# Two-layer decoder trunk on one core: four closing blocks of 512 columns, shared early chunks, and a residual in written order

## The chip, the cores and the metric

The kernel runs on one core of a Trainium2 chip. The metric is device time in microseconds (us) of one execution; a lower number is better.

## The reference, cut to what matters

The reference is a decoder trunk of two layers over 256 rows of 2048 numbers. Each layer adds three sub-layers to the running sum `h`: a token mixing, a cross attention over 256 memory rows, and a gated feed-forward. Each sub-layer normalises its input and its output.

```python
D_MODEL, SEQ, DEPTH, MEM_LEN = 2048, 256, 2, 256
FFN_HIDDEN = 5632

def rms_norm(x, g):
    xf = x.astype(jnp.float32)
    y = xf * lax.rsqrt(jnp.mean(xf * xf, axis=-1, keepdims=True) + EPS)
    return (y * g.astype(jnp.float32)).astype(x.dtype)
```

Of a layer, in words: `mix` is three groups of attention heads and a gating, joined to 2048 columns and multiplied by `w_out` (2048 by 2048); then `h = h + rms_norm(mix, mix_post_g)`. The cross attention takes keys and values from the normalised memory (`x_wkv`), queries from `rms_norm(h, x_pre_g)`, four heads of 128, and closes with `x_wo` (512 by 2048); then `h = h + rms_norm(cross, x_post_g)`. The feed-forward is `silu(h w_g) * (h w_u)` with 5632 hidden columns, closes with `f_w_down` (5632 by 2048), and is added in the same manner.

## The kernel before, in words

Every float32 product is computed as three products of a 32-bit format with a shorter mantissa: each operand is split into a part `hi` (ScalarE copies it, L206) and a rest `lo` (VectorE subtracts, L207), and PE, the matmul engine, adds hi·hi, hi·lo and lo·hi. Weights come by DMA from SyncE's queue into three buffers `raw` of 1 MB. `splits()` cuts each into **chunks** of 1024 columns, of which `hi` and `lo` have three buffers each. One chunk of a 512-column block holds two row groups `k` of 128, and gives 24 matmuls of 256 columns where the weights stand still (`mm_t`), or 12 of 512 where the activations do (`mm_n`).

`weights()` (L358) hands out chunks. After each it calls `prefetch()`, which writes out the splits of later chunks, so that up to three are in hand, and `pump()`, which advances every generator in `side` by one step: that is how the normalisations and attentions are laid beside the matmuls. The order on an engine is set by a scheduler's own estimate of time, save within `tc.manual_schedule(engines={DVE, ACT})`, where VectorE (DVE) and ScalarE (ACT) take the order in which the code is written and PE is still placed by the estimate. `begin(gen, n, at)` (L638) opens that mode at step `at` of a generator's first `n` steps; it ends with the block of weights that is being read. In that mode `pump()` comes before `prefetch()` (L371 to L375).

The closing projections `w_out`, `x_wo` and `f_w_down` run over `TAIL`, five blocks of columns, with two accumulators each. The first block of `w_out` takes its row groups in the order `MIX_FIRST`: first the ten that exist early (`m6`, and columns 6 and 7), then six whose mixing outputs are split late by `chunks()` into `mx`.

`residual()` (L585) follows a closing projection: it evaluates the last block's squares (`evac`), takes the inverse root of the row sums (`row_rsqrt`, on DVE), adds the scaled block to `H` (`add`, L604), transposes pairs of 128-column groups of `H` on PE (`turn_x`, tile `xtp`), and splits them into the next sub-layer's `x` (`split_x`: `hi` by L212 on ACT, `lo` by L213 on DVE). With `bare` false (after the mixing) it runs beside the matmuls of the memory's keys, `acc<-mh,...` and `acc<-ml,...`: 8 chunks K0 to K7 of 24 matmuls, after which the query matmuls Q0 to Q7 need `x`. There the order is the scheduler's, and half of the sums go to ACT and POOL (`beside`). With `bare` true (after cross attention and feed-forward) warming matmuls stand first, and DVE and ACT run in the written order.

```python
            if ramp:
                pump()
                prefetch()
                ...
            else:
                prefetch(3 if not hold or n < nk else 2)
                pump()
```

Of the kernel before, what the change touches and what calls it, by code (L numbers as in the profile page):

```python
# [10 lines left out]
F32 = mybir.dt.float32  # L11
# [10 lines left out]
P = 128  # L22
# [36 lines left out]
def trunk(ctx: ExitStack, tc, a, onehot, out):  # L59
# [14 lines left out]
    ps3 = ctx.enter_context(tc.tile_pool(name="ps3", bufs=2, space=PSUM))  # L74


    nc.gpsimd.memset(pc.tile([P, 8], F32, name="half_pc"), 0.0)


    ident = cp.tile([P, P], F32, name="ident")  # L80
# [175 lines left out]

        return lambda k0, n: w3d[k0 * P:(k0 + n) * P, :, c0:c0 + cols].rearrange("(k p) c f -> p k c f", p=P)

    TAIL = ((0, 512), (512, 512), (1024, 512), (1536, 256), (1792, 256))
    MIX_FIRST = ((8, 4), (0, 4), (6, 2), (4, 2), (12, 4))  # L260

    def plan():


        def spec(dram, nk, cols, loads=None, sub=None):
            per = 2048 // cols
            loads = loads or [(k, min(per, nk - k)) for k in range(0, nk, per)]
            return dram, nk, cols, loads, sub or (4 if cols <= 256 else 2 if cols <= 512 else 1)

        for l in range(L):  # L270
            w_in, w_out = a["w_in"][l], a["w_out"][l]
            w_qi = a["b_w_qidx"][l].rearrange("r g d -> r (g d)")
            w_uq = a["b_w_uq"][l].rearrange("r h d -> r (h d)")
            w_uk = a["b_w_uk"][l].rearrange("r h d -> r (h d)")
            w_uv = a["b_w_uv"][l].rearrange("r h d -> r (h d)")
            x_wkv = a["x_wkv"][l].rearrange("k c h e -> k c (h e)")
            x_wq = a["x_wq"][l].rearrange("k h e -> k (h e)")
            x_wo = a["x_wo"][l].rearrange("h e d -> (h e) d")
            yield spec(rows(w_in, C_CU, 512), KD, 512, None if l else [(0, 1), (1, 3), (4, 4), (8, 4), (12, 4)])
# [12 lines left out]
            w_qk = w_in[:, 0:1536].rearrange("k (c f) -> k c f", c=2)  # L292
            for h in range(0, 6, 2):
                yield spec(pairs(w_qk, h * P, 256), KD, 512)
            yield spec(rows(w_in, C_CV, 512), KD, 512)
            for i, (c0, n) in enumerate(TAIL):
                yield spec(rows(w_out, c0, n), KD, n, MIX_FIRST if i == 0 else None)
            yield spec(rows(x_wkv[:, 0, :], 0, 512), KD, 512)
            yield spec(rows(x_wq, 0, 512), KD, 512)
            for g in range(2):  # L300
                yield spec(rows(x_wkv[:, 1, :], g * 256, 256), KD, 256)
            for c0, n in TAIL:
                yield spec(rows(x_wo, c0, n), 4, n, None, 2)
            nh = FH // P // 2
            for hf in range(2):
                for j in range(0, nh, 2):
                    yield spec(pairs(a["f_w_gu"][l], (hf * nh + j) * P, 256), KD, 512)
                wd = a["f_w_down"][l][hf * nh * P:(hf + 1) * nh * P, :]
                for c0, n in TAIL:
                    yield spec(rows(wd, c0, n), nh, n)  # L310
# [85 lines left out]
                mm(outs[b], hi[:, cs[b]], xl[k], False, last)  # L396
        return tiles

    def mm_n(nk, cols, xh, xl, hold=False):

        xh, xl = ([x[:, k, :] for k in range(nk)] if not isinstance(x, list) else x for x in (xh, xl))
        tiles = [acc.tile([P, 512], F32, tag="acc", name="acc") for _ in range(2)]
        for n, k, hi, lo in weights(nk, cols, hold):
            for t in range(2):
                o = tiles[t][:, :cols]
                h, lw = xh[k][:, t * P:(t + 1) * P], xl[k][:, t * P:(t + 1) * P]
                mm(o, h, hi, n == 0, False)
                mm(o, h, lo, False, False)
                mm(o, lw, hi, False, n == nk - 1)
        return tiles  # L410

    def warm(n):
# [172 lines left out]
    def residual(og, ss, evac, nxt, res, bare, off):  # L585
# [5 lines left out]
        r = row_rsqrt(ss)  # L591
        if bare:
            warm(38)
        yield
        res["x"] = xh, xl, _ = new_x("x", off)

        def add(c, n, beside=False):
            f = slice(c * P, (c + n) * P)
            for t in range(2):
                if beside:  # L600
                    nc.scalar.activation(og[:, t, f], og[:, t, f], AF.Copy, scale=r[:, t:t + 1])
                    nc.gpsimd.tensor_tensor(H[:, t, f], H[:, t, f], og[:, t, f], op=ALU.add)
                else:
                    nc.vector.scalar_tensor_tensor(H[:, t, f], og[:, t, f], r[:, t:t + 1], H[:, t, f],  # L604
                                                   op0=ALU.mult, op1=ALU.add)

        def turn(c):
            split_x(turn_x(H, c), c, xh, xl, nxt)


        add(0, 2)
        p = turn_x(H, 0)
# [1 line left out]
        split_x(p, 0, xh, xl, nxt)  # L614
        turn(2)
        add(4, 2)
        if bare:
            prefetch()
        rest()
        add(6, 2)  # L620
        yield
        turn(4)
        yield
        turn(6)
        add(8, 4, not bare)
        yield
        turn(8)
        yield
        turn(10)
        add(12, 4, not bare)  # L630
        yield
        turn(12)
        yield
# [11 lines left out]
            next(gen)  # L645
        start(gen)

    def project_out(nk, xh, xl, og, gain, add=False, first=None):

# [3 lines left out]
        for g, (c0, cols) in enumerate(TAIL):  # L653
            last = g == len(TAIL) - 1
            if gain.shape[0] == P:
                gb = gain[:, c0:c0 + cols]
            else:
                gb = wk.tile([P, 512], F32, tag="gb", name="gb", bufs=2)[:, :cols]
                nc.gpsimd.dma_start(gb, gain[c0:c0 + cols].partition_broadcast(P))
            tiles = mm_n(nk, cols, *(first if first and g == 0 else (xh, xl)), hold=last)  # L660

            def evac(tiles=tiles, g=g, c0=c0, cols=cols, gb=gb, last=last):
                for t in range(2):
                    d, p = og[:, t, c0:c0 + cols], tiles[t][:, :cols]
                    if add:
                        nc.vector.tensor_tensor(d, p, d, op=ALU.add)
                        square(d, ss[:, t, g:g + 1])
                        if not last:
                            nc.gpsimd.tensor_tensor(d, d, gb, op=ALU.mult)
                    else:  # L670
                        square(p, ss[:, t, g:g + 1])
                        if not last:
                            nc.vector.tensor_tensor(d, p, gb, op=ALU.mult)
                if not last:
                    return

                def rest():
                    for t in range(2):
                        d, p = og[:, t, c0:c0 + cols], tiles[t][:, :cols]
                        if add:  # L680
                            nc.gpsimd.tensor_tensor(d, d, gb, op=ALU.mult)
                        else:
                            nc.vector.tensor_tensor(d, p, gb, op=ALU.mult)
                return rest
            if last:
                return ss, evac
            later(evac)

    def last_residual(og, ss, evac):
# [5 lines left out]
        for t, f in pieces[:3]:  # L695
            summed[t, f.start] = p = acc.tile([P, 512], F32, tag="acc", name="hsum")
            mm(p, ident, H[:, t, f], True, False)
        dg = spread(r)
        rest()
        for t, f in pieces[:3]:  # L700
            mm(summed[t, f.start], dg[:, t, :], og[:, t, f], False, True)
        for i in (3, 0, 4, 1, 5, 2, 6, 7):
            t, f = pieces[i]
            p = summed.get((t, f.start))
            if p is not None:
                nc.scalar.activation(H[:, t, f], p, AF.Copy)
# [22 lines left out]
    in_raw.append(next(loads))  # L729
    fetch_x(256, 256)  # L730
    in_raw.append(next(loads))
    fetch_x(512, 512)
    in_raw.append(next(loads))
    warm(12)
    for _ in g0:
        pass
    cur = {}
    begin(initial(cur), 2, -1)


    for l in range(L):
# [377 lines left out]
        og = xp.tile([P, 2, D], F32, tag="x", name="og")  # L1119
        pool = {}  # L1120

        at = used[0]

        def turn_memory():
            while used[0] == at or any(g.__name__ in ("last_heads", "chunks") for g in side):
# [4 lines left out]
            pool["m"] = mh, ml = [kp.tile([P, KD, S], F32R, name=n) for n in ("mh", "ml")]  # L1130
            yield from memory(kp, mh, ml, l)
        start(turn_memory())
        oss, evac = project_out(KD, mxx[:, 0], mxx[:, 1], og, a["mix_post_g"][l], first=first)


        kp = pool["kp"]
# [3 lines left out]
        kX = kp.tile([P, 4, 256], F32, name="kX")  # L1140
        vX = kp.tile([P, 2, 512], F32, name="vX")
        nx = {}
        begin(residual(og, oss, evac, ("x_pre_g", l), nx, False, 64), 2, -1)
        t_k = mm_t(KD, [P] * 4, mh, ml)

        def k_out():
# [142 lines left out]
```

## Time and profile before

| | us |
|---|---|
| median of three runs | 2426.8 |
| lowest and highest | 2422.76, 2428.68 |
| the profiled execution's own time | 2425.12 |
| its span, first to last instruction | 2423.4 |
| PE busy in it | 2389.2 (99%) |
| DVE, ACT, POOL busy | 1412.6, 1188.7, 201.9 |

The busy share of PE is modelled from the starts of pipelined matmuls, so the distance between starts tells more than a duration: a row `start us, us, ... xN [idle before <-releaser]` gives the first start of N like instructions in a row, and how long the engine had been idle before it and for whom.

### The profile page before, as it was taken

How to read it: one execution, taken by the hardware profiler on the slowest of the kernel's cores; microseconds unless marked ns; L12 is line 12 of the kernel's file. 1: busy time of each engine (PE TensorE's matmuls, PEld its weight loads, DVE VectorE, ACT ScalarE, POOL GpSimd, SP SyncE). 2: the span in 40 equal slices, each digit the busy share in tenths (PEclk: the TensorE clock that was granted, in tenths of full speed). 3: DMA queues.
4: the chain of work that ended last, by engine and by line, in shares of the span. 5: the costliest groups of instructions: out<-in, count | busy, mean ns of one | idle time of the engine just before them, and what ended most of it. 6: DMA issues, size and time to landing. Idle time of an engine off the chain costs nothing.

```text
span 2423.4 us, 42616 instructions
## 1 busy us (share of the span) xinstructions
PE 2389.2 (99%) x17741; PEld 2249.2 (93%) x17741; DVE 1412.6 (58%) x2129; ACT 1188.7 (49%) x1764; POOL 201.9 (8%) x177
## 2 busy tenths in 40 slices
PE   9999999999999999999999999999999999999998
PEld 8899789999998999998999997999999989999987
DVE  5686766665554455555466767666655544555554
ACT  5655545554444444444455655455544444444443
POOL 0010131000000000000100102100000000000001
PEclk9999999999999999999999999999999999999999
DMA  7755475455655565555554555644555555555553
GB/s 250 242 170 157 164 252 176 157 176 196 197 195 194 187 195 193 192 192 192 190 173 132 187 156 189 219 157 157 190 194 192 191 192 190 192 195 196 193 191 131
DMA packets 356757, 453.27 MB, mean 187 GB/s; under 512 B 11290, under 2 KB 275412, under 8 KB 356052
## 3 DMA queue, kind: packets, MB, share of 16 engines
q1 hardware_dynamic: 354836, 443.45, 55.9%
q0 software_dynamic: 1248, 6.29, 0.8%
q8 instruction: 139, 2.28, 0.4%
q10 hardware_dynamic: 480, 0.80, 0.1%
q14 instruction: 54, 0.44, 0.1%
HBM read 444.72 MB, written 5.79 MB: 186 GB/s over the span
## 4 chain that ended last, share of the span: by engine, by line
PE 91%; DVE 4%; ACT 2%; DMA 2%; issue 1%; SPq 0%; POOL 0%; ACTq 0%; POOLq 0%; DVEq 0%
PE acc L201 86%; DVE lo L207 2%; ACT hi L206 1%; PE xtp L564 1%; PE ixp L201 1%; ACT sqj L550 1%; PE lga L201 1%; DMA m<-in_mem_dram 1%; DVE H L604 1%; DMA H<-in_x_dram 0%; DVE mx L207 0%; PE warm L416 0%; DMA lp<-in_a_lambda_dram 0%; PE pvb L201 0%; PE lgx L201 0%
## 5 line engine op out<-in xcount | busy, mean ns | idle before, releaser
L207 DVE TENSOR_TENSOR lo<-raw,hi 128x1024 fp32r<-128x1024 f32 (+2 forms) x839 | 1000.9, 1194 | 870.7 <-ACT hi L206 868.4
L206 ACT ACTIVATE hi<-raw 128x1024 fp32r<-128x1024 f32 (+2 forms) x839 | 861.0, 1027 | 1037.7 <-PE acc L201 954.7
L201 PE MATMUL acc<-x,hi 128*128 128x256 f32 (+1 forms) x7360 | 1270.0, 277 | 0.0
L201 PEld LDWEIGHTS acc<-x,hi 128*128 128x128 f32 (+1 forms) x7360 | 1111.2, 188 | 2.8 <-issue 2.7
L201 PE MATMUL acc<-x,lo 128*128 128x256 f32 x3680 | 889.5, 278 | 6.8 <-DVE lo L207 4.6
L201 PEld LDWEIGHTS acc<-x,lo 128*128 128x128 f32 x3680 | 690.1, 188 | 13.4 <-DVE lo L207 6.1
L201 PE MATMUL acc<-hi,hx 128*128 128x512 f32 (+1 forms) x1760 | 452.6, 347 | 0.0
L201 PEld LDWEIGHTS acc<-hi,hx 128*128 128x128 f32 x1760 | 308.5, 189 | 41.7 <-issue 0.2
L201 PE MATMUL acc<-lo,hx 128*128 128x512 f32 (+1 forms) x880 | 304.9, 347 | 0.0
L201 PEld LDWEIGHTS acc<-lo,hx 128*128 128x128 f32 x880 | 166.7, 189 | 20.5 <-issue 0.2
L1243 POOL TENSOR_TENSOR g<-g,u 128x512 f32<-128x512 f32 x44 | 76.6, 1741 | 1131.3 <-ACT g L1241 1131.3
L201 PE MATMUL acc<-hi,mx 128*128 128x512 f32 (+1 forms) x576 | 148.1, 345 | 7.9 <-DVE mx L207 4.0
L201 PEld LDWEIGHTS acc<-hi,mx 128*128 128x128 f32 x576 | 99.6, 190 | 21.8 <-DVE mx L207 5.1
L201 PE MATMUL acc<-hi,x 128*128 128x384 f32 (+1 forms) x384 | 109.3, 360 | 0.0
L201 PE MATMUL acc<-lo,mx 128*128 128x512 f32 (+1 forms) x288 | 98.4, 343 | 0.1
L201 PEld LDWEIGHTS acc<-hi,x 128*128 128x128 f32 x384 | 70.1, 188 | 8.3 <-issue 3.3
L201 PE MATMUL acc<-lo,x 128*128 128x384 f32 (+1 forms) x192 | 69.7, 363 | 0.0
L212 ACT ACTIVATE x<-xtp,gT 128x256 fp32r<-128x256 f32 x96 | 39.5, 470 | 48.7 <-PE xtp L564 48.7
L201 PEld LDWEIGHTS acc<-lo,mx 128*128 128x128 f32 x288 | 54.6, 190 | 7.0 <-DVE lo L207 1.0
L213 DVE SCALAR_TENSOR_TENSOR x<-xtp,gT,x 128x256 fp32r<-128x256 f32 x96 | 41.6, 478 | 16.1 <-ACT x L212 15.9
L201 PE MATMUL acc<-hi,cx 128*128 128x512 f32 (+1 forms) x160 | 42.7, 352 | 0.0
L201 PEld LDWEIGHTS acc<-lo,x 128*128 128x128 f32 x192 | 36.1, 188 | 3.9 <-issue 1.3
(247 smaller groups left out, 1878.4 us busy)
## 6 DMA issues: line engine op xcount, KB each, us to landing
raw<-in_f_w_gu_dram SPq DMA_DIRECT2D x352, 512.0 KB, 4.5
raw<-in_f_w_down_dram SPq DMA_DIRECT2D x76, 1024.0 KB, 5.1
raw<-in_w_out_dram SPq DMA_DIRECT2D x30, 1024.0 KB, 5.4
raw<-in_w_in_dram SPq DMA_DIRECT2D x48, 512.0 KB, 4.7
raw<-in_w_in_dram SPq DMA_DIRECT2D x23, 1024.0 KB, 5.3
raw<-in_x_wkv_dram SPq DMA_DIRECT2D x16, 1024.0 KB, 4.9
raw<-in_w_in_dram SPq DMA_DIRECT2D x12, 960.0 KB, 5.1
raw<-in_x_wq_dram SPq DMA_DIRECT2D x8, 1024.0 KB, 5.2
```

Source lines behind the costliest of these rows:

```text
L201: return nc.tensor.matmul(o, lhsT=lhsT, rhs=rhs, start=start, stop=stop, skip_group_check=True)
L206: nc.scalar.activation(hi, src, AF.Copy)
L207: eng.tensor_tensor(lo, src, hi.bitcast(F32), op=ALU.subtract)
L212: nc.scalar.activation(hi, src, AF.Copy, scale=scale)
L213: nc.vector.scalar_tensor_tensor(lo, src, scale, hi.bitcast(F32), op0=ALU.mult, op1=ALU.subtract)
L550: nc.scalar.activation(q[:, :src.shape[-1]], src, AF.Square, accum_out=red)
L564: nc.tensor.transpose(p[:, t * P:(t + 1) * P], src[:, t, (c + j) * P:(c + j + 1) * P], ident)
L604: nc.vector.scalar_tensor_tensor(H[:, t, f], og[:, t, f], r[:, t:t + 1], H[:, t, f], op0=ALU.mult, op1=ALU.add)
L1243: nc.gpsimd.tensor_tensor(g, g, u, op=ALU.mult)
```

## The change: what it does

There are six edits. `TAIL` has four blocks of 512 instead of three of 512 and two of 256. The first two blocks of `w_out` run their ten early row groups one after the other, and then their six late ones, on four accumulators; the memory's transposes begin one block later. In `mm_n`, the last two row groups of a projection's last block run first for rows 0 to 127, then for 128 to 255. `residual()` after the mixing runs in written order: the last block's gain first, then for each of eight pairs the sum, the transposes and the split, one pair a step; the share of ACT and POOL is gone. `initial()`, which splits the input, runs in written order too, and the first weights come in smaller loads, three of them ahead of `H`'s third part. The last block's gain is multiplied on DVE. Some paddings change, by which `cx` and small work tiles move within SBUF.

```diff
-    TAIL = ((0, 512), (512, 512), (1024, 512), (1536, 256), (1792, 256))
-    MIX_FIRST = ((8, 4), (0, 4), (6, 2), (4, 2), (12, 4))
+    TAIL = ((0, 512), (512, 512), (1024, 512), (1536, 512))
+
+    MIX_EARLY, MIX_LATE = ((8, 4), (0, 4), (6, 2)), ((4, 2), (12, 4))
...
-            yield spec(rows(w_in, C_CU, 512), KD, 512, None if l else [(0, 1), (1, 3), (4, 4), (8, 4), (12, 4)])
+            yield spec(rows(w_in, C_CU, 512), KD, 512, None if l else [(0, 1), (1, 1), (2, 2), (4, 4), (8, 4), (12, 4)])
...
-            for i, (c0, n) in enumerate(TAIL):
-                yield spec(rows(w_out, c0, n), KD, n, MIX_FIRST if i == 0 else None)
+            for part, n in ((MIX_EARLY, 10), (MIX_LATE, 6)):
+                for c0, cols in TAIL[:2]:
+                    yield spec(rows(w_out, c0, cols), n, cols, part)
+            for c0, cols in TAIL[2:]:
+                yield spec(rows(w_out, c0, cols), KD, cols)
...
+        end = []
+        for w in weights(nk, cols, hold):
+            if hold and w[0] >= nk - 2:
+                end.append(w)
+                if w[0] < nk - 1:
+                    continue
+                for t in range(2):
+                    for w in end:
+                        step(t, *w)
+            else:
+                for t in range(2):
+                    step(t, *w)
...
         r = row_rsqrt(ss)
         if bare:
             warm(38)
-        yield
+            yield
         res["x"] = xh, xl, _ = new_x("x", off)
 
-        def add(c, n, beside=False):
+        def add(c, n):
             f = slice(c * P, (c + n) * P)
             for t in range(2):
-                if beside:
-                    nc.scalar.activation(og[:, t, f], og[:, t, f], AF.Copy, scale=r[:, t:t + 1])
-                    nc.gpsimd.tensor_tensor(H[:, t, f], H[:, t, f], og[:, t, f], op=ALU.add)
-                else:
-                    nc.vector.scalar_tensor_tensor(H[:, t, f], og[:, t, f], r[:, t:t + 1], H[:, t, f],
-                                                   op0=ALU.mult, op1=ALU.add)
+                nc.vector.scalar_tensor_tensor(H[:, t, f], og[:, t, f], r[:, t:t + 1], H[:, t, f],
+                                               op0=ALU.mult, op1=ALU.add)
...
+        if not bare:
+            rest()
+            yield
+            for c in range(0, KD, 2):
+                add(c, 2)
+                turn(c)
+                yield
+            yield from pre_norm(res)
+            return
...
+        warm(24)
         dg = spread(r)
-        rest()
...
     in_raw.append(next(loads))
+    in_raw.append(next(loads))
     fetch_x(512, 512)
-    in_raw.append(next(loads))
...
-    begin(initial(cur), 2, -1)
+    begin(initial(cur), 2, 0)
...
-        oss, evac = project_out(KD, mxx[:, 0], mxx[:, 1], og, a["mix_post_g"][l], first=first)
+        early = [mm_n(10, cols, *first, more=True) for _, cols in TAIL[:2]]
+        oss, evac = project_out(KD, mxx[:, 0], mxx[:, 1], og, a["mix_post_g"][l], early=early)
...
-        begin(residual(og, oss, evac, ("x_pre_g", l), nx, False, 64), 2, -1)
+        begin(residual(og, oss, evac, ("x_pre_g", l), nx, False, 64), 1, 0)
...
-        cx = kp.tile([P, 2080], F32R, name="cx")[:, 32:].rearrange("p (a h t) -> p a h t", a=2, h=4)
+        cx = kp.tile([P, 2064], F32R, name="cx")[:, 16:].rearrange("p (a h t) -> p a h t", a=2, h=4)
```

Three places in the order of instructions follow. On DVE beside the memory's keys, before (`H` is the sum, `x` the split's rest of a transposed half pair, `lo` the rest of a weight chunk):

```order
L604 SCALAR_TENSOR_TENSOR H<-og,rs_r,H 128x256 x8
L207 TENSOR_TENSOR lo<-raw,hi 128x1024 x2
L213 SCALAR_TENSOR_TENSOR x<-xtp,gT,x 128x256 x4
L207 TENSOR_TENSOR lo<-raw,hi 128x1024 x2
L213 SCALAR_TENSOR_TENSOR x<-xtp,gT,x 128x256 x4
L207 TENSOR_TENSOR lo<-raw,hi 128x1024
```

and after:

```order
L694 TENSOR_TENSOR og<-acc,gb 128x512 x2
L619 SCALAR_TENSOR_TENSOR H<-og,rs_r,H 128x256 x2
L213 SCALAR_TENSOR_TENSOR x<-xtp,gT,x 128x256 x2
L207 TENSOR_TENSOR lo<-raw,hi 128x1024
L619 SCALAR_TENSOR_TENSOR H<-og,rs_r,H 128x256 x2
L213 SCALAR_TENSOR_TENSOR x<-xtp,gT,x 128x256 x2
L207 TENSOR_TENSOR lo<-raw,hi 128x1024
```

The sums no longer stand in one piece, and each chunk's `lo` now stands behind the `x` of one pair; the first `lo` here is that of K3, the next that of K4, up to that of Q2.

On PE, where the first pairs are transposed beside the keys, before (four `xtp` are one pair; these rows lie in the first half of K3):

```order
L201 MATMUL acc<-mh,lo 128x256
L564 MATMUL xtp<-ident,H 128x128 x2
L201 MATMUL acc<-mh,hi 128x256
L201 MATMUL acc<-ml,hi 128x256
L564 MATMUL xtp<-ident,H 128x128 x2
L201 MATMUL acc<-ml,hi 128x256
L564 MATMUL xtp<-ident,H 128x128 x2
L201 MATMUL acc<-ml,hi 128x256 x2
L564 MATMUL xtp<-ident,H 128x128 x2
```

and after, the last rows of K3 and the first two of K4:

```order
L201 MATMUL acc<-mh,hi 128x256
L201 MATMUL acc<-ml,hi 128x256
L583 MATMUL xtp<-ident,H 128x128 x2
L201 MATMUL acc<-ml,hi 128x256 x2
L583 MATMUL xtp<-ident,H 128x128 x2
L201 MATMUL acc<-ml,hi 128x256
L201 MATMUL acc<-mh,lo 128x256
L201 MATMUL acc<-mh,hi 128x256
```

One pair now stands at the end of each chunk, with one `acc<-ml,hi` of its own chunk behind it; the first pair stands alone between K2 and K3.

On SyncE at the start, before:

```order
L714 DMA H<-in_x_dram 128x2x256
L323 DMA raw<-in_w_in_dram 128x3x512
L714 DMA H<-in_x_dram 128x2x512
L323 DMA raw<-in_w_in_dram 128x4x512
L714 DMA H<-in_x_dram 128x2x512 x2
L323 DMA raw<-in_w_in_dram 128x4x512
L105 DMA gload<-in_x_pre_g_dram 32x128
```

and after:

```order
L735 DMA H<-in_x_dram 128x2x256
L327 DMA raw<-in_w_in_dram 128x512
L327 DMA raw<-in_w_in_dram 128x2x512
L735 DMA H<-in_x_dram 128x2x512 x3
L105 DMA gload<-in_x_pre_g_dram 32x128
```

The first load of four row groups (`128x4x512`), which stood ahead of `gload` twice, now stands behind nine small loads, of which `gload` is the first.

## Rows read from the trace of the kernel before

**Rows 1.** The page: PE's busy time, and the chain that ended last, by engine.
```profile
PE 2389.2 (99%) x17741; PEld 2249.2 (93%) x17741; DVE 1412.6 (58%) x2129; ACT 1188.7 (49%) x1764; POOL 201.9 (8%) x177
PE 91%; DVE 4%; ACT 2%; DMA 2%; issue 1%; SPq 0%; POOL 0%; ACTq 0%; POOLq 0%; DVEq 0%
```
**Rows 2.** PE's waits: for whom, us in total, times, longest us.
```profile
PE acc L201 <- DVE lo L207: 10.0, 9, 2.7
PE acc L201 <- DVE mx L207: 4.0, 2, 2.0
PE acc L201 <- ACT mx L206: 3.9, 2, 1.9
PE hsum L201 <- DVE dg L487: 2.7, 1, 2.7
```
**Rows 3.** Timeline of PE: down projection, block of 512, then of 256.
```profile
1111.62 0.39 PE L201 MATMUL acc<-hi,hx 128*128 128x512 f32 x1
...
1114.80 0.39 PE L201 MATMUL acc<-hi,hx 128*128 128x512 f32 x1
...
2407.72 0.40 PE L201 MATMUL acc<-hi,hx 128*128 128x256 f32 x2
...
2410.24 0.28 PE L201 MATMUL acc<-hi,hx 128*128 128x256 f32 x1
```
**Rows 4.** Timeline of PE, first block of `w_out`: its late chunks, layer 0.
```profile
288.20 0.50 PE L201 MATMUL acc<-hi,mx 128*128 128x512 f32 x1 [1.95 <-ACT mx L206]
...
292.07 0.97 PE L201 MATMUL acc<-hi,mx 128*128 128x512 f32 x3 [2.04 <-DVE mx L207]
```
**Rows 5.** Timeline of PE beside the memory's keys, layer 0.
```profile
383.92 0.63 PE L201 MATMUL acc<-ml,hi 128*128 128x256 f32 x4
387.23 0.55 PE L201 MATMUL acc<-mh,lo 128*128 128x256 f32 x1 [2.68 <-DVE lo L207]
```
**Rows 6.** Windows: PE, PEld, DVE, ACT, POOL busy (x); granted clock; DMA share; GB/s.
```profile
387.10:390.40 3.30, 3.17 (x15) 3.20 (x16) 3.30 (x6) 0.52 (x2) 0.00 (x0) 0.50 0.17 60
390.50:394.00 3.50, 3.50 (x33) 3.50 (x32) 1.56 (x2) 2.23 (x5) 0.00 (x0) 1.00 0.63 241
...
2414.60:2419.00 4.40, 4.08 (x6) 1.70 (x6) 3.48 (x6) 1.45 (x3) 0.00 (x0) 0.61 0.62 233
```
**Rows 7.** Timeline of DVE beside the memory's keys.
```profile
378.55 7.40 DVE L604 SCALAR_TENSOR_TENSOR H<-og,rs_r,H 128x256 f32<-128x256 f32 x8
385.87 2.35 DVE L207 TENSOR_TENSOR lo<-raw,hi 128x1024 fp32r<-128x1024 f32 x2
```
**Rows 8.** Timeline: one pair in written order after cross attention; PE, ACT, DVE.
```profile
488.50 0.38 PE L564 MATMUL xtp<-ident,H 128*128 128x128 f32 x2
...
488.80 0.84 ACT L212 ACTIVATE x<-xtp,gT 128x256 fp32r<-128x256 f32 x2 [2.98 <-PE xtp L564]
489.53 1.06 ACT L206 ACTIVATE hi<-raw 128x1024 fp32r<-128x1024 f32 x1
...
489.31 0.88 DVE L213 SCALAR_TENSOR_TENSOR x<-xtp,gT,x 128x256 fp32r<-128x256 f32 x2 [0.46 <-ACT x L212]
490.62 1.23 DVE L207 TENSOR_TENSOR lo<-raw,hi 128x1024 fp32r<-128x1024 f32 x1 [0.43 <-ACT hi L206]
```
**Rows 9.** The start: SyncE's queue and PE (timeline), the loads' landing (page).
```profile
7.23 0.47 SPq L323 DMA_DIRECT2D raw<-in_w_in_dram  x1
7.74 3.90 SPq L105 DMA_DIRECT2D gload<-in_x_pre_g_dram  x1
14.88 0.32 SPq L134 DMA_DIRECT2D oh<-in_onehot_dram  x1
...
21.22 4.05 SPq L323 DMA_DIRECT2D raw<-in_w_in_dram  x3
...
18.21 0.36 PE L201 MATMUL acc<-x,lo 128*128 128x256 f32 x1
...
raw<-in_w_in_dram SPq DMA_DIRECT2D x23, 1024.0 KB, 5.3
```

More of the change, by code (lines that the diff above doesn't have):

```diff
@@ L74, in trunk @@
     ps3 = ctx.enter_context(tc.tile_pool(name="ps3", bufs=2, space=PSUM))
-    nc.gpsimd.memset(pc.tile([P, 8], F32, name="half_pc"), 0.0)
+    nc.gpsimd.memset(pc.tile([P, 24], F32, name="gap"), 0.0)
     ident = cp.tile([P, P], F32, name="ident")
@@ L397, in mm_t, with mm_n, step @@
         return tiles
-    def mm_n(nk, cols, xh, xl, hold=False):
+    def mm_n(nk, cols, xh, xl, hold=False, into=None, more=False):
         xh, xl = ([x[:, k, :] for k in range(nk)] if not isinstance(x, list) else x for x in (xh, xl))
[L402 to L409, printed above, removed]
+        tiles = into or [acc.tile([P, 512], F32, tag="acc", name="acc") for _ in range(2)]
+        def step(t, n, k, hi, lo):
+            o = tiles[t][:, :cols]
+            h, lw = xh[k][:, t * P:(t + 1) * P], xl[k][:, t * P:(t + 1) * P]
+            mm(o, h, hi, n == 0 and not into, False)
+            mm(o, h, lo, False, False)
+            mm(o, lw, hi, False, n == nk - 1 and not more)
+        end = []
[10 more added lines that the diff above has]
+                    step(t, *w)
         return tiles
@@ L616, in residual @@
         add(4, 2)
-        if bare:
-            prefetch()
+        prefetch()
         rest()
@@ L624, in residual @@
         turn(6)
-        add(8, 4, not bare)
+        add(8, 4)
         yield
@@ L629, in residual @@
         turn(10)
-        add(12, 4, not bare)
+        add(12, 4)
         yield
@@ L646, in begin, with project_out @@
         start(gen)
-    def project_out(nk, xh, xl, og, gain, add=False, first=None):
+    def project_out(nk, xh, xl, og, gain, add=False, early=()):
         ss = sm.tile([P, 2, len(TAIL)], F32, tag="sso", name="sso", bufs=2)
@@ L659, in project_out, with scaled @@
                 nc.gpsimd.dma_start(gb, gain[c0:c0 + cols].partition_broadcast(P))
-            tiles = mm_n(nk, cols, *(first if first and g == 0 else (xh, xl)), hold=last)
+            if g < len(early):
+                tiles = mm_n(6, cols, [xh[:, k, :] for k in range(KD)], [xl[:, k, :] for k in range(KD)], into=early[g])
+            else:
+                tiles = mm_n(nk, cols, xh, xl, hold=last)
             def evac(tiles=tiles, g=g, c0=c0, cols=cols, gb=gb, last=last):
+                def scaled(t, eng):
+                    d, p = og[:, t, c0:c0 + cols], tiles[t][:, :cols]
+                    if add:
+                        eng.tensor_tensor(d, d, gb, op=ALU.mult)
+                    else:
+                        nc.vector.tensor_tensor(d, p, gb, op=ALU.mult)
                 for t in range(2):
@@ L666, in evac @@
                         nc.vector.tensor_tensor(d, p, d, op=ALU.add)
[L667 to L684, printed above, removed]
+                    square(d if add else p, ss[:, t, g:g + 1])
+                    if not last:
+                        scaled(t, nc.gpsimd)
+                return lambda: [scaled(t, nc.vector) for t in range(2)]
             if last:
@@ L703, in last_residual @@
             t, f = pieces[i]
+            if i == 2:
+                rest()
             p = summed.get((t, f.start))
@@ L1120, in trunk @@
         pool = {}
-        at = used[0]
+        at = used[0] + 1
         def turn_memory():
-            while used[0] == at or any(g.__name__ in ("last_heads", "chunks") for g in side):
+            while used[0] <= at or any(g.__name__ in ("last_heads", "chunks") for g in side):
                 yield
```

## The prediction

> **What bounds the kernel now.** I read the page first: PE is busy 99% of the span, and the chain that ended last is PE's for 91% [rows 1]. So only two kinds of edit can move the time: fewer or cheaper starts on PE, and waits of PE that go or come. PE's waits then show where the waits of before are [rows 2]: VectorE's `lo` and the mixing's two splits lead, and the end of the kernel has one of 2.7 us. The timelines place them. In the first block of `w_out` PE stands still twice, for 1.95 and 2.04 us, until two late mixing outputs are split [rows 4]. Beside the memory's keys it stands still once, for 2.68 us, for the `lo` of chunk K4 [rows 5], because DVE was in one run of eight sums that took 7.40 us and the `lo` stood behind it [rows 7]. After that wait the granted clock was 0.50, that is 1.2 GHz, for about 3.3 us, and then 1.00 again [rows 6]. Layer 1 repeats both patterns, as the counts of two show [rows 2].
>
> **The blocks of 512.** The down projection starts 14 matmuls of 512 columns between 1111.62 and 1114.80, 227 ns each, and 21 of 256 between 2407.72 and 2410.24, 120 ns each [rows 3]. Two of 256 cost 240, one of 512 costs 227: 13 ns a pair. A pair disappears in `w_out` 16 x 6 x 2 = 192 times and in `f_w_down` 22 x 6 x 2 x 2 = 528 times: 720 x 13 ns = -9.4 us. `x_wo` has 48 more pairs and moves its input within SBUF; by the same row I estimate -0.4 (0 to -1). Sum -9.8. The row shows a price for two starts of 13 ns above one of twice the width. The Trainium skill ("TensorE: Matmul & The Clock Gate", section "Wait — 56ns, not 53.3ns?") gives a fixed part of about 2.5 ns per warm matmul beside its columns; by it the 768 pairs would save 1.9 us, and the sum below would be 8 us higher. The row decides, since it is of these tiles.
>
> **The shared early chunks.** The late rows were ready at 288.20 and 292.07 [rows 4], with early work ending near 286.2. Block 1's ten early row groups put 10 x 6 x 227 ns = 13.6 us more ahead of them, so that the late work starts near 299.8, 7.7 us after the last input. Both waits go; with the restart of the pipeline they cost 2.2 and 2.3 us, so -4.5 a layer, -9.0 in all. Next late is nothing on PE there. If that cover were gone, -9.0 becomes 0. The memory's transposes start a block later; they have two further blocks of 96 matmuls of 512 (21.8 us each) before the keys, so I cost that at 0.
>
> **The residual beside the keys.** First what goes. Without the run of eight sums the wait for K4 goes: from the last four matmuls at 383.92, 113 ns each, PE would have gone on at 384.37 and went on at 387.23 [rows 5], 2.86 us; the half clock behind it cost half of about 3.3 us, 1.65 [rows 6]. That is -4.5 a layer, -9.0 in all.
>
> Then what comes. In after, DVE's order is sum, `x`, `lo`, sum, `x`, `lo`: the `lo` of K3 stands behind the `x` of pair 0, that of K4 behind pair 1, and so on to Q2 behind pair 7. DVE can't do an `x` before the pair's transposes, and on PE these stand at the end of the chunk ahead, with one matmul behind them in most cases. So PE finishes a chunk, having only just given DVE and ACT what they need, and must wait for the whole chain. The timeline has this chain once [rows 8], in the same order, after cross attention: last transposes at 488.50, ACT's `x` 488.80, ACT's `hi` 489.53, DVE's `x` 489.31, DVE's `lo` 490.62 for 1.23 us, so ready at 491.85: 3.35 us after the transposes' start. PE covers 0.14 us with the transposes and 0.11 for each matmul behind them, of which there are 0 to 5 in the eight places. A wait is thus 2.6 to 3.2 us, mean 2.95; eight a layer, sixteen in all: +47. Bounds: 16 x 2.4 = +38 if ACT's copies start 0.5 us earlier than there, 16 x 3.4 = +54 if a square of ACT falls into the chain. Behind each waiting `x` on DVE only the next `lo` and the next sum are queued, and PE waits for that `lo`. The sums cost nothing: two take an estimated 0.9 us (as two of DVE's `x` in [rows 8], of the same width), beside the chunk's matmuls.
>
> **The clock after these waits.** The three waits of 2.7 us idle and more (K4 in each layer, `dg` at the end) were each followed by half clock or a window at 0.61 [rows 2, 6]; the four of about 2 us in the mixing [rows 2] were not. Mine lie between and above, but with only 2.7 us of matmuls between them, which no row shows. From 0 to 16 x 1.65 = +26; I take half of them at 1.5: +12. [...]
>
> **The start.** Before, the weights of row groups 4 to 7 were issued ahead of `gload`, with PE on them at 18.21 [rows 9]. In after they stand behind the nine small loads, which ran from 7.74 to about 21 in before (the next `raw` at 21.22; `oh`, the fifth, at 14.88). With less data queued ahead of them I put the issue near 15, the landing 5.3 us later [rows 9], `hi` and `lo` 2.3 us after that (1.06 and 1.23 [rows 8]): about 22.6, against 18.21. +4.4, rounded to +5 as two later loads follow it; bounds +2 (issue at 12.5) and +10 (issue at 21.2).
>
> **Other edits.** The gain on DVE replaces two POOL multiplications that ended before `dg` was ready; the reordered last two row groups let the squares of rows 0 to 127 start 6 matmuls, 1.4 us, earlier, at the mixing, cross and feed-forward closings; PE has warming matmuls or key chunks there. Together 0, bounds -3 and +2.
>
> **The sum**, from the profiled 2425.1, which lies 1.7 below the median: -9.8 -9.0 -9.0 +47 +12 +5 = +36.2: 2461.
>
> **Rivals.** *PE never waits beside the keys* (faster). After cross attention the same written order ran without a wait of PE: the chain of 3.35 us [rows 8] lay beside a chunk's matmuls. DVE's own work a pair is 0.88 + 0.88 + 1.23 = 3.0 us against 24 x 113 ns + 4 transposes = 3.1 us on PE; so if the transposes came a chunk's length earlier than the `lo` is needed, nothing waits. It decides at 2.7 us of matmuls between the last transposes and the chunk that needs the `lo`; the order shows 0 to 0.6. Time: 2425.1 - 9.8 - 9.0 - 9.0 + 5 = 2402. *Half waits* (no change): if each wait is about 1.4 us, too short for the clock to fall (the mixing's two didn't), 16 x 1.4 = 22 + 5 - 27.8 gives 2425. It would take a chain of 1.8 us, and the `hi` and `lo` alone are 2.3 [rows 8], so it speaks against itself. *No half clock*: the waits as forecast, PE at 2.4 GHz: 2449. *Half clock every time*: 2476. *The widths pay as by the fixed part alone*: 2469.
>
> **Chances.** Forecast, between 2452 and 2468: 0.46. No half clock: 0.16. Half clock every time: 0.20. Widths without gain: 0.04. PE never waits: 0.06. Half waits: 0.04. A start or first pair that costs over 10 us more, above 2481: 0.04. The range reaches from the lower bound of the case without half clock (2449 - 5) to the upper of that with it each time: 2444 to 2481. About 0.3% (7 us) is what a measurement of this kernel can tell from no change. Faster by more than that 0.06, within it 0.04, slower 0.90.
>
> **What would show it.** In after, the timeline of PE beside the keys should show eight waits a layer, released by `lo`, each behind `xtp` and a matmul or so; PE's waits for `lo` should come to 45 us or more in place of 10.0, those for the mixing's splits should be gone, and the granted clock of these 50 us should be 0.6 to 0.9. Blocks of down projection should show 227 ns throughout. PE's start of row group 4 should be near 23. If PE waits there less than 20 us in all, the step on the chain is wrong; if PE waits 47 and the time is below 2450, the clock's; if the windows of blocks show another distance than 227, the widths'.

## The result

The changed kernel is slower: a median of 2488.8 us in four runs (2485.16 to 2490.25) against 2426.7, a ratio of 1.0256 with a 95% interval of 1.0238 to 1.0274. The forecast was 2461, with a range of 2444 to 2481: the sign was right, the size was not. The profiled run took 2485.16 us, its span is 2483.4, that is 60.0 longer than before's. It is the shortest of the four, at a mean granted clock of 0.992, where the other three had 0.988 to 0.989; so what is read from it below on the clock is probably too little for the median.

To see where, I cut both spans at the first matmul of each stretch. The table is worked out from these starts, both layers summed; the right column is the forecast's sum, sorted in the same way.

| stretch | before, us | after, us | difference | forecast |
|---|---|---|---|---|
| start to the first `w_out` matmul, layer 0 | 271.3 | 278.3 | +7.0 | +5 |
| `w_out` | 198.6 | 185.0 | -13.5 | -11.5 |
| keys and queries, with the residual | 105.1 | 160.6 | +55.4 | +50 |
| feed-forward, first halves (gate and up) | 489.9 | 489.8 | -0.1 | 0 |
| down projections and what follows them | 502.5 | 494.2 | -8.3 | -6.9 |
| feed-forward, second halves (gate and up) | 478.8 | 497.5 | **+18.7** | **0** |
| all other stretches, and behind the last matmul | | | +0.8 | -0.4 |

One line is wrong by more than all others together: the second halves of the feed-forward. No edit touches their instructions, and no wait appears there.

PE's waits in after (for whom, us in total, times, longest) answer to [rows 2]:

```profile
PE acc L201 <- DVE lo L207: 57.7, 26, 5.7
PE acc L201 <- ACT x L212: 1.4, 6, 0.2
PE hsum L201 <- DVE dg L506: 0.9, 1, 0.9
```

The mixing's two waits are gone, `dg`'s fell from 2.7 to 0.9, and `lo` went from 10.0 to 57.7 us. The next rows are the timeline of PE at the end of K3 and the start of K4 (to be read beside [rows 5]), and then those of ACT and DVE in the same two chunks (beside [rows 8]):

```profile
387.38 0.38 PE L583 MATMUL xtp<-ident,H 128*128 128x128 f32 x2
387.51 0.49 PE L201 MATMUL acc<-ml,hi 128*128 128x256 f32 x2
387.84 0.38 PE L583 MATMUL xtp<-ident,H 128*128 128x128 f32 x2
387.98 0.36 PE L201 MATMUL acc<-ml,hi 128*128 128x256 f32 x1
391.33 0.55 PE L201 MATMUL acc<-mh,lo 128*128 128x256 f32 x1 [3.00 <-DVE lo L207]
...
388.15 0.84 ACT L212 ACTIVATE x<-xtp,gT 128x256 fp32r<-128x256 f32 x2 [1.50 <-PE xtp L583]
388.88 1.06 ACT L206 ACTIVATE hi<-raw 128x1024 fp32r<-128x1024 f32 x1
...
388.66 0.87 DVE L213 SCALAR_TENSOR_TENSOR x<-xtp,gT,x 128x256 fp32r<-128x256 f32 x2 [3.18 <-ACT x L212]
389.96 1.22 DVE L207 TENSOR_TENSOR lo<-raw,hi 128x1024 fp32r<-128x1024 f32 x1 [0.43 <-ACT hi L206]
```

From the pair's last transposes at 387.84 to the end of `lo` at 391.18 are 3.34 us; the chain taken from the other residual had 3.35. Such a wait stands at all 14 places ahead of K3 to K7, Q0 and Q1, of 2.5 to 3.1 us by the profile, and shorter ones ahead of Q2. Counted as the forecast counted them, from start to start less the usual distance, they are 2.7 to 3.3 us each, and all 16 together 50.2 us of delay against the 47 forecast. The granted clock in this stretch (window; PE, PEld, DVE, ACT, POOL; clock; DMA share; GB/s), layer 0 and 1:

```profile
372.60:453.40 80.80, 57.00 (x422) 55.31 (x421) 38.86 (x78) 29.47 (x52) 0.54 (x1) 0.92 0.32 108
1597.20:1677.00 79.80, 57.21 (x421) 55.73 (x420) 38.80 (x78) 29.53 (x52) 0.00 (x0) 0.89 0.33 106
```

The stretch lost 64.4 us (55.4 and the 9.0 that went, a figure of the forecast); 50.2 are the waits, so 14.2 are left for the clock, against 12 forecast. After 7 of the 16 waits the matmuls came 213 ns apart, after the others 113 to 118. Counted from these starts, what the matmuls behind the seven waits took above 113 ns each is 13.4 us.

And the second halves: matmuls of `x`, the counts in equal windows, of before (window and its length, then PE and PEld busy (x), DVE, ACT, granted clock, DMA share, GB/s):

```profile
920.00:1080.00 160.00, 160.00 (x1415) 160.00 (x1414) 0.00 (x0) 0.00 (x0) 1.00 0.58 192
2130.00:2280.00 150.00, 150.00 (x1326) 150.00 (x1325) 0.00 (x0) 0.00 (x0) 1.00 0.59 193
```

and of after:

```profile
920.00:1080.00 160.00, 160.00 (x1361) 160.00 (x1360) 0.00 (x0) 0.00 (x0) 1.00 0.58 185
2130.00:2280.00 150.00, 150.00 (x1276) 150.00 (x1276) 0.00 (x0) 0.00 (x0) 1.00 0.58 189
```

PE is busy all the time in both, the granted clock is 1.00 in both, and there are 54 matmuls fewer in 160 us: 113.1 ns from start to start before, 117.6 after. The instructions and their order are the same. Busy shares, waits and the clock are all blind to this; only the distance of starts shows it.

### The profile page after: what moved, and what is told of

Its sections match the earlier page's. It is cut to its first block, busy times and chain, and to the rows that moved or that the text cites. A ratio compares the mean times of both kernels' runs of the same rounds, so it can differ in the third digit from the quotient of the medians.

```text
span 2483.4 us, 41047 instructions
## 1 busy us (share of the span) xinstructions
PE 2413.2 (97%) x16997; PEld 2244.9 (90%) x16997; DVE 1410.7 (57%) x2129; ACT 1181.8 (48%) x1720; POOL 185.1 (7%) x159
## 4 chain that ended last, share of the span: by engine, by line
PE 92%; DVE 3%; ACT 3%; DMA 2%; issue 1%; SPq 0%; POOL 0%; ACTq 0%; POOLq 0%; DVEq 0%
PE acc L201 87%; DVE lo L207 2%; ACT hi L206 1%; ACT x L212 1%; ACT sqj L569 1%; PE ixp L201 1%; DMA m<-in_mem_dram 1%; PE xtp L583 1%; PE lga L201 1%; PE warm L435 1%; DMA H<-in_x_dram 0%; PE pva L201 0%; PE pvb L201 0%; DMA raw<-in_w_in_dram 0%; PE ptp L443 0%
## 5 line engine op out<-in xcount | busy, mean ns | idle before, releaser
L201 PE MATMUL acc<-x,hi 128*128 128x256 f32 (+1 forms) x7360 | 1294.4, 280 | 0.0
L201 PE MATMUL acc<-hi,hx 128*128 128x512 f32 x1408 | 434.1, 389 | 0.0
L201 PEld LDWEIGHTS acc<-hi,hx 128*128 128x128 f32 x1408 | 264.2, 188 | 55.0 <-issue 0.2
L201 PE MATMUL acc<-lo,hx 128*128 128x512 f32 x704 | 274.3, 390 | 0.0
L201 PEld LDWEIGHTS acc<-lo,hx 128*128 128x128 f32 x704 | 132.2, 188 | 27.5 <-issue 0.2
L201 PE MATMUL acc<-hi,mx 128*128 128x512 f32 x384 | 120.7, 391 | 0.0
L201 PEld LDWEIGHTS acc<-hi,mx 128*128 128x128 f32 x384 | 71.9, 188 | 14.8 <-DVE mx L207 0.2
L201 PE MATMUL acc<-lo,mx 128*128 128x512 f32 x192 | 75.0, 391 | 0.0
L201 PE MATMUL acc<-mh,lo 128*128 128x256 f32 x128 | 37.4, 318 | 29.2 <-DVE lo L207 29.2
L201 PEld LDWEIGHTS acc<-mh,lo 128*128 128x128 f32 x128 | 28.3, 221 | 31.1 <-issue 31.0
```

What stands on the lines that cost most here:

```text
L201: return nc.tensor.matmul(o, lhsT=lhsT, rhs=rhs, start=start, stop=stop, skip_group_check=True)
```

## Experiments

Times are medians; the ratio is to the kernel before, with its 95% interval. Each run's profile was cut into the same stretches.

| run | us | ratio | interval |
|---|---|---|---|
| a_warm | 2468.1 | 1.0170 | 1.0139 to 1.0201 |
| b_mid256 | 2446.5 | 1.0081 | 1.0052 to 1.0110 |
| a_probe | 2485.9 | a single run | |
| b_tail4 | 2425.8 | 1.0003 | 0.9994 to 1.0012 |
| b_tail4_gap | 2439.5 | 1.0050 | 1.0027 to 1.0073 |
| a_oldres | 2429.2 | 1.0014 | 1.0002 to 1.0025 |
| a_split_first | 2480.0 | 1.0219 | 1.0189 to 1.0249 |
| a_sum_ahead | 2433.2 | 1.0028 | 1.0016 to 1.0040 |
| a_oldstart | 2479.6 | 1.0220 | 1.0199 to 1.0240 |
| a_oldloads | 2485.0 | 1.0241 | 1.0211 to 1.0271 |
| best_old | 2405.3 | 0.9912 | 0.9896 to 0.9929 |
| best_both | 2403.6 | 0.9910 | 0.9894 to 0.9927 |

### The distance of starts: a_warm, b_mid256, a_probe

My theory was that the distance is a rhythm which PE takes over from the matmuls just ahead and keeps; the rival was that it comes with the weight buffers or accumulators, since four blocks have 44 chunks where five had 45.

```diff
+            if hf:
+                warm(4)
             for j in range(0, nh, 2):
                 start(act(mm_t(KD, [P] * 4, xh, xl), j, hh, hl))
```

> The changed kernel with four warming matmuls of 256 columns put ahead of the second half of each feed-forward, nothing else. In the changed kernel the 2112 matmuls of that half start 118 ns apart, in the one before 113 ns. Theory 1 (the distance is a rhythm that PE takes over from what it did just before, 227 ns matmuls of 512 columns there, 120 ns ones of 256 before, and keeps until something breaks it): with the four ahead the half falls to 113 ns, the half takes 239.5 us in place of 248.8, and the kernel is 18 us shorter, about 2469. Rival (the distance comes with the weights' chunk buffers or the accumulators, which the changed count of chunks, 44 in place of 45, shifts): 118 ns stays, the time is about 2489.

In a_warm (timeline of PE) the four matmuls stand between the last of 512 columns and the first of `x`:

```profile
878.53 0.64 PE L435 MATMUL warm<-wz 128*128 128x256 f32 x4
879.00 0.28 PE L201 MATMUL acc<-x,lo 128*128 128x256 f32 x1
```

and the window over `x` has this count:

```profile
920.00:1080.00 160.00, 160.00 (x1414) 160.00 (x1414) 0.00 (x0) 0.00 (x0) 1.00 0.60 195
```

1414 matmuls in the window, where before had 1415; each second half takes 239.4 us, and half a microsecond of added work takes 20.7 us off the median. In b_mid256 only the order of blocks changes:

```diff
-    TAIL = ((0, 512), (512, 512), (1024, 512), (1536, 256), (1792, 256))
+    TAIL = ((0, 512), (512, 256), (768, 256), (1024, 512), (1536, 512))
```

> The kernel before with its five closing blocks in another order, the two of 256 columns second and third, two of 512 last; nothing else. The count of chunks, buffers and accumulators stays. Theory 1 (rhythm taken over from the matmuls ahead): the second half of each feed-forward now follows matmuls of 512 and runs at 118 ns, 9.4 us longer each, 18.7 in all: about 2445. Rival (buffers and accumulators): 113 ns stays, about 2427.

The same window of b_mid256:

```profile
920.00:1080.00 160.00, 160.00 (x1361) 160.00 (x1361) 0.00 (x0) 0.00 (x0) 1.00 0.57 186
```

1361, as in after, and 2446.5 us against the 2445 expected: the kernel before gets the same loss from the order of its blocks alone, with the count of chunks as it was. The rival on buffers falls. a_probe puts other things into four stretches of the changed kernel:

```diff
+            if hf:
+                warm(l + 1)
             for j in range(0, nh, 2):
+                if hf == 0 and j == 12:
+                    wide(1 if l == 0 else 4)
```

(`wide(n)` issues n matmuls of 512 columns on the warming tile.)

> The changed kernel with four additions that look for what sets the distance of the feed-forward's 256-column matmuls, one in each of four stretches of 240 us: one warming matmul of 256 columns ahead of layer 0's second half, two ahead of layer 1's; one matmul of 512 columns in the middle of layer 0's first half, four in that of layer 1's. Theory (the distance is taken over from the matmuls just before): the first halves run at 113 ns up to the added matmuls and at 118 ns behind them, at least behind four; of the second halves the one with two is at 113 ns, the one with one may be at either. Rival (only what the warming tile or its wait does counts): no change in the first halves.

Windows of a_probe, matmuls of `x`: layer 0's first half ahead of and behind one wide matmul (at 648.19), layer 1's ahead of and behind four (from 1876.22 on), then the second halves behind one and behind two warming matmuls:

```profile
560.00:640.00 80.00, 80.00 (x708) 80.00 (x707) 0.00 (x0) 0.00 (x0) 1.00 0.60 199
660.00:740.00 80.00, 80.00 (x708) 80.00 (x707) 0.00 (x0) 0.00 (x0) 1.00 0.60 198
1790.00:1870.00 80.00, 80.00 (x709) 80.00 (x708) 0.00 (x0) 0.00 (x0) 1.00 0.60 198
1890.00:1970.00 80.00, 80.00 (x682) 80.00 (x681) 0.00 (x0) 0.00 (x0) 1.00 0.56 189
890.00:1050.00 160.00, 160.00 (x1361) 160.00 (x1360) 0.00 (x0) 0.00 (x0) 1.00 0.58 189
2130.00:2290.00 160.00, 160.00 (x1414) 160.00 (x1413) 0.00 (x0) 0.00 (x0) 1.00 0.59 194
```

One wide matmul changes nothing (708 in 80 us, 113 ns, on both sides of it), four put the rest of the half to 117 ns (709, then 682 in 80 us). One warming matmul leaves the second half slow, two bring it back. So the distance can be made longer in mid-stretch and shorter ahead of a stretch, and then stays, here for over 100 us. Each dose was tried once, in one run, and the two doses of a kind in different layers.

### Is it the width alone? b_tail4 and b_tail4_gap

```diff
-    TAIL = ((0, 512), (512, 512), (1024, 512), (1536, 256), (1792, 256))
+    TAIL = ((0, 512), (512, 512), (1024, 512), (1536, 512))
```

> The kernel before with four closing blocks of 512 columns and nothing else. Theory: by the stretches of the runs so far the blocks save 1.75 us in each of four down projections, 1.2 in each w_out and 0.2 in each x_wo, 10 us in all, and cost 9.4 us in each of two second halves of the feed-forward, which then follow matmuls of 512: about 2435, slower than before although no wait was added. Rival (my own step in the prediction: 13 ns for each pair and nothing else): about 2417.

This expectation failed: 2425.8, no difference. The second halves ran at 113 ns behind matmuls of 512. But the first down projection took 120.9 us in place of the changed kernel's 119.7. With four entries in place of five the array of row sums is smaller, the tiles behind it moved, and with them `hx`, the down projection's input. The changed kernel makes up for that with 16 more floats, 64 bytes, of padding. So I added them:

```diff
-    nc.gpsimd.memset(pc.tile([P, 8], F32, name="half_pc"), 0.0)
+    nc.gpsimd.memset(pc.tile([P, 24], F32, name="gap"), 0.0)
```

> The kernel before with four closing blocks of 512, as b_tail4, and with the 64 bytes of padding that the changed kernel adds, so that the down projection's input hx stands where it does in both kernels (in b_tail4 the smaller array of row sums moved it). In b_tail4 the matmuls of hx came 226 to 232 ns apart, unevenly, and the second halves behind them ran at 113 ns. Theory (the rhythm is taken over from the matmuls ahead: from hx at 227 ns, evenly, it locks at 118 ns, from other distances it may fall to 113): here hx is at 227, the second halves at 118 ns and 248.8 us, and the time is about 2435. Rival (something else of the changed kernel locks it, and 512 columns alone do not): 113 ns, about 2416.

Windows of b_tail4: matmuls of `hx` in 113 us of the first down projection, then of `x` in the window used above:

```profile
732.00:845.00 113.00, 113.00 (x495) 92.70 (x495) 0.68 (x1) 0.61 (x1) 1.00 0.56 189
...
920.00:1080.00 160.00, 160.00 (x1414) 160.00 (x1413) 0.00 (x0) 0.00 (x0) 1.00 0.58 192
```

and the same of b_tail4_gap:

```profile
732.00:845.00 113.00, 113.00 (x500) 93.62 (x499) 0.68 (x1) 0.62 (x1) 1.00 0.58 192
...
920.00:1080.00 160.00, 160.00 (x1361) 160.00 (x1361) 0.00 (x0) 0.00 (x0) 1.00 0.56 185
```

Where `hx` lies such that its matmuls come faster (500 in the window against 495), the following 2112 come slower. The operands of those 2112 did not move: in both programs `x` and the weights' `hi` and `lo` have the same addresses in SBUF. Of what PE reads in the two stretches only `hx` moved, the operand that stands still in the down projection: it starts at byte 161632 of a partition in b_tail4 and at 161696, 64 bytes further, in b_tail4_gap, before and after. So it is not the width alone, but what PE was doing, width and place together, when it came to `x`. The four blocks alone cost 13 us with the padding (2439.5, about 2435 expected) and nothing without it, and the slower `hx` gave the better kernel.

### The residual beside the keys: a_oldres, a_split_first, a_sum_ahead

a_oldres is the changed kernel with before's residual and its `begin(..., 2, -1)`.

> The changed kernel with the old residual after the mixing (order by the scheduler, part of the sums on ACT and POOL). Theory (the written order costs 64 us, and its removal brings the old wait of 2.9 us and its half clock back, 9 us for both layers): 55 us shorter, about 2433, with the other 6 us of the loss from the start and the feed-forward's second halves against the gains of the blocks and the mixing. Rival (the longer start or the 512-wide blocks cost more than the traces' sums tell): above 2445.

2429.2: of the 62 us, the written order of this residual is worth 59.6. PE waits once a layer in the keys, for 2.4 us, where before waited 2.7, and without half clock behind it. Next I tried to mend the written order. First by splitting ahead:

```diff
             if ramp:
+                if first_split:
+                    prefetch()
                 pump()
                 prefetch()
...
```

(`first_split` is set only around the residual after the mixing.)

> The changed kernel with one thing in another order beside the memory's keys: the next weight chunk's split is written ahead of the pair's transposes and not behind them, so each lo stands one pair further back. Theory (the chain from a pair's transposes to the next lo is what PE waits for): each lo has a chunk of 24 matmuls more, 2.7 us, against a chain of 3.35, so the eight waits a layer of 2.7 to 3.3 us fall to 0.6 or less, the half clock goes with them, and about 55 of the 64 us of that stretch go: about 2432. Rival (DVE's own work of 3.0 us a pair is too much for a chunk of 2.7 us): the waits only halve, about 2460.

The timeline of PE ahead of K4, and the row of PE's waits for `lo`:

```profile
384.04 0.38 PE L585 MATMUL xtp<-ident,H 128*128 128x128 f32 x2
...
387.53 0.55 PE L201 MATMUL acc<-mh,lo 128*128 128x256 f32 x1 [3.00 <-DVE lo L207]
```

```profile
PE acc L201 <- DVE lo L207: 51.6, 23, 6.0
```

A miss: 8.8 us in place of 57. Seven waits a layer stayed, each about as long as before (2.4 to 3.1 us), one chunk later. In DVE's order the sum of the next pair stands behind the split, so with the split everything that follows from the sum moved back too: PE's transposes again stood in the last matmuls ahead of the `lo` that needs them. The edit moved the distance between split and transposes on DVE, but not on PE, where it counts. So I moved the sum instead:

```diff
-            for c in range(0, KD, 2):
-                add(c, 2)
-                turn(c)
+            add(0, 2)
+            for c in range(0, KD, 2):
+                p = turn_x(H, c)
+                if c + 2 < KD:
+                    add(c + 2, 2)
+                split_x(p, c, xh, xl, nxt)
                 yield
```

> The changed kernel with each pair's sum written one pair ahead, before the split of the pair that has just been transposed; nothing else. PE's order then has pair p+1's transposes at the end of the chunk at whose end pair p's stood. Theory (PE waits because the transposes of the pair that a lo stands behind come in the last matmuls of the chunk ahead of that lo; splitting first did not help because in DVE's order the next sum, and so the next transposes, moved back with the split): seven of the eight waits a layer go, the first of 3.3 us stays, and about 55 of the 64 us of the stretch go: about 2433. Rival (DVE's loop of sum, x and lo takes longer than a chunk): seven waits of 1 us or more a layer stay, 2445 or more.

The same two views of a_sum_ahead, ahead of K3:

```profile
381.36 1.03 PE L583 MATMUL xtp<-ident,H 128*128 128x128 f32 x8
385.07 0.36 PE L201 MATMUL acc<-mh,lo 128*128 128x256 f32 x1 [2.68 <-DVE lo L207]
```

```profile
PE acc L201 <- DVE lo L207: 19.4, 17, 5.9
```

2433.2, as expected. Two pairs are transposed ahead of K3 (the eight `xtp`), the one wait of 2.7 us there stays, and of the other seven two of 0.3 us a layer are left. The chain and all instructions are those of the changed kernel; only the order differs, each sum one pair earlier on DVE and with it the transposes on PE. That shows the cause: not that the order is written, but a chain of 3.3 us that began at the end of each chunk.

### The start: a_oldstart, a_oldloads

a_oldstart has before's first loads and before's order of the input's splits; a_oldloads has only the code of the loads back.

> The changed kernel with the loads and the order of the start as before; nothing else. Theory (the start costs 7 us because the weights of row groups 4 to 7 are issued behind nine small loads): PE has no wait of 5.9 us near 20 us, and the time is 7 us shorter, about 2482. Rival (the input's splits in written order cost it, not the loads' order, or the time is made up later): within 3 us of 2489.

> The changed kernel with the first loads as before, and the input's splits still in written order. Theory (the small loads ahead of row groups 4 to 7 are what costs the start): PE's wait of 5.9 us near 20 us goes and the mixing begins 7 us earlier than in the changed kernel, about 2481. Rival (the written order of the splits costs it): the wait stays, about 2488.

In after (timeline of SyncE's queue and of PE), SyncE gets to row groups 4 to 7 at 16.02, and PE to them at 25.68, where before had 18.21 [rows 9]:

```profile
16.02 1.69 SPq L327 DMA_DIRECT2D raw<-in_w_in_dram  x3
...
25.68 0.58 PE L201 MATMUL acc<-x,lo 128*128 128x256 f32 x1 [5.75 <-DVE lo L207]
```

The first `w_out` matmul comes at 278.3 in after, 274.7 in a_oldloads and 270.6 in a_oldstart (before: 271.3); by the medians a_oldloads is 3.9 us shorter than after and a_oldstart 9.2. These figures are good to 2 or 3 us only: best_old and best_both (below), with the start of a_oldstart, come to `w_out` at 273.2 and 272.7. With the old loads the wait of 5.75 us is gone, but PE's transposes wait for the input's loads. From the list of PE's waits of a_oldloads:

```profile
PE xtp L583 <- DMA H<-in_x_dram: 4.8, 2, 3.4
```

So the order of the loads costs part of the 7 us, some 4, and the rest comes with the written order of the splits; neither expectation was met in full. That second part is not the splits alone: in a_oldloads the second load of four row groups still stands behind the nine small ones (issued at 18.91, in a_oldstart at 7.14), and best_both too waits 1.9 us for `H`. How the rest divides is not shown.

### Two kernels that beat both: best_old, best_both

best_old is the changed kernel with the old residual, the old start and `warm(4)` ahead of the second halves. best_both keeps the written order, with a_split_first and a_sum_ahead together and the last block's gain after the fourth pair.

> The changed kernel with the old residual after the mixing, the old start, and four warming matmuls ahead of each second half of the feed-forward; what stays of the change are the blocks of 512, the shared early chunks, the end and the paddings. By the stretches of the runs so far: mixing 7.0 shorter in each layer, the keys 1.4, cross attention 0.4, the down projections 3.9 in each: 25 us shorter than the kernel before, about 2402. Rival (a gain in one stretch is given back as another distance of starts or a later wait): 2410 or more.

> The changed kernel with the old start, four warming matmuls ahead of each second half of the feed-forward, and the written order beside the keys put so that each thing has a chunk of room: the next weights' split ahead of the pair's transposes, each pair's sum one pair ahead, the last block's gain after the fourth pair. By the order, pair 0's transposes stand 12 matmuls ahead of K4, whose lo stands behind pair 0: a wait of about 1.4 us before K4, none after. That is 3 us a layer less than with the old residual: about 2399 against 2405. Rival (DVE's 3.0 us a pair, and 1.3 more in one step for the gain, come out as waits in the middle): 2405 or more.

The row of best_both's waits for `lo`, and its timeline of PE at K4:

```profile
PE acc L201 <- DVE lo L207: 8.1, 13, 1.3
```

```profile
380.35 0.36 PE L201 MATMUL acc<-mh,lo 128*128 128x256 f32 x1 [1.29 <-DVE lo L207]
```

One wait of 1.3 us ahead of K4 and two of 0.4 us are left in each layer, without half clock behind them. 2405.3 and 2403.6 are 21 to 22 us less than before; the two are too near to be told apart by their intervals. By the stretches the keys and queries of best_both are 1.1 us a layer shorter than best_old's (51.7 against 52.8), not the 3 expected. In a_oldres the same old residual, which there had no half clock behind its wait, takes 51.2. So whether the mended written order is better than the old residual hangs on the clock, and these runs don't show it.

## Why the prediction was right or wrong

- **The blocks of 512.** The price per pair was right: b_tail4_gap saves 1.4 us in each `w_out` and 1.75 in the first down projection of each layer, against 1.25 and 1.7. The blocks show 227 ns throughout. The rival in which the widths pay by a fixed part alone, 1.9 us in all, fell.
- **The step that failed** stands in the prediction's part on the blocks of 512, unspoken: that a change of width costs or saves only on the matmuls whose width it changes. The sum had no term for the 4224 matmuls of the feed-forward's second halves that follow these blocks; it put them at nothing without a reason. The runs showed 4.4 ns more for each, 18.7 us, because PE keeps the distance that it came with: a_warm takes the loss away, and b_mid256 and b_tail4_gap bring it into the kernel before. The trace of before had the two distances side by side (113 and 118 ns in the keys), and the prediction did not ask what decides between them. With this term the sum would have been 2480; the small misses of the other terms make up the 5 us to the profiled run, which lies 3.7 below the median. None of the signs of being wrong that the prediction names would have shown this one.
- **Shared early chunks.** Right: both waits gone. `w_out` shrank by 6.8 us a layer, of which 1.4 are the blocks; 5.4 against 4.5.
- **The waits beside the keys.** Right in place, count and cause; 50.2 against 47. The chain taken from another stage was 3.35 us, and here 3.34.
- **The clock.** 13.4 to 14.2 against 12, half clock behind 7 of 16 waits where I had put 8. That it would be about half was a choice between the two bounds that no row bore out, so this nearness is luck. The Trainium skill ("TensorE: Matmul & The Clock Gate", section "HAM oscillation — how this bites in real kernels") tells of a kernel in which every wait of some 3 to 5 us between groups of matmuls was followed by a cold clock. Here, with waits of 2.0 to 3.1 us, it was less than half of them. The length of the wait, by which the prediction set the three of 2.7 us apart from the four of 2 us, does not decide it here: waits of 3.0 us are found with and without half clock behind them, and the wait of 2.4 us for K4 had it in both layers of best_old and in none of a_oldres. What decides it stays open.
- **The start.** +7.0 against +5 and inside its bounds. The issue came at 16.02, near the 15 put down, but PE reached row group 4 at 25.68 and not near 23; and there is a second cause that I had not priced and that is not fully resolved, what follows from the splits in written order.
- **Other edits.** `dg`'s wait fell by 1.8 us and the rows behind the last matmul gave most of it back: about 0, as forecast.
- **The range.** Without the missed term, the sum of the measured stretches would be 2466 in the profiled run, inside the range; with it, outside.

## What to carry to other kernels

Where PE is the bound and never waits, still compare the distance of its starts between two traces, stretch by stretch: 4 ns on thousands of equal matmuls was a third of this loss, and neither waits, busy shares nor the granted clock show it. When work is moved into a written order, find where on each engine the first link of the chain will stand, not only the last; a `lo` one chunk ahead of its use helps nothing if the transposes behind which it is queued come at the end of that chunk. And when an edit changes the size of a tile, list the tiles behind it that move: here 64 bytes were worth 13 us.

## What the runs showed of the hardware that I had not expected

Matmuls of 256 columns over the same tile, with the same weights and at a granted clock of 1.00, run at either 113 or 118 ns from start to start, and stay at it for up to 249 us. Four matmuls of 512 columns ahead switch to the slower, one doesn't; two of 256 from another tile switch back, one doesn't (each tried once, in a_probe; four of 256 switched back in both layers of a_warm, best_old and best_both). 64 bytes in the place of the preceding input decide it as well (b_tail4 and b_tail4_gap). Why PE has two such rhythms no run here tells; that it takes them over from what it did just before is shown by a_warm, b_mid256 and a_probe.
